# Decay exponents of the bidirectional SSD made by matmuls of 16 split rows, one exponential for both directions, and chunk rows loaded one chunk ahead

## The chip, the cores and the metric

The kernel runs on one core of one Trainium2 chip. The metric is the device time of one execution in microseconds, taken as the median over runs. The engines are PE (TensorE; PEld is its weight load), DVE (VectorE), ACT (ScalarE), POOL (GpSimd) and SP, which issues most DMAs.

## The reference

One encoder layer over 1280 tokens of width 1024 (a prompt of 256 and a sample of 1024, handled as one array of 10 chunks of 128 tokens). After a norm and an input projection, an S5 branch and a bidirectional Mamba-2 SSD branch run beside each other; gates merge them, and an MLP and a last norm follow. What the change touches is the SSD scan, run once forward and once backward over flipped inputs:

```python
da_cs = jnp.cumsum(dt * a.reshape(M2_GROUPS, k), axis=2)      # within a chunk of 128
xdt = x * dt[..., None]
lower = jnp.tril(jnp.ones((M2_CHUNK, M2_CHUNK), dtype=bool))[:, :, None, None]
seg = da_cs[:, :, :, None] - da_cs[:, :, None, :]
decay = jnp.exp(jnp.where(lower, seg, -jnp.inf))              # 128 x 128 for every head
cb = jnp.einsum('bclgn,bcsgn->bclsg', cm, bm)
y_diag = jnp.einsum('bclsg,bclsgk,bcsgkp->bclgkp', cb, decay, xdt)
...
y_off = jnp.einsum('bclgn,bcgkpn,bclgk->bclgkp', cm, prev, jnp.exp(da_cs))
```

There are 4 groups of 6 heads of 64 channels, and a state of 128.

## The kernel before, in words

Instructions are written in program order with priorities, and the framework's scheduler fixes at build time in which order each engine takes them. An engine runs its own list in order; a wait of one instruction holds up all that stand behind it. The same goes for the queue of DMAs on SP and that on ACT.

In order of time: the input projection for the S5 inputs, the S5 branch between further projection tiles (to about 560 us in the profiled execution), dt_proc (lines 344 to 421, near 540 to 605 us), the SSD stage, the two halves of the GLU (lines 624 to 657), merge and residual (to 1705 us), then the MLP.

**The SSD stage** runs over 4 groups j and 10 chunks k, 40 chunks in all. chunk_in (line 471) loads four 128x128 blocks of a chunk, transposes them on PE (line 477) and builds the backward state; chunk and chunk_out (lines 487 and 515) compute a chunk's output. The projection tiles for later groups and for gates (lists LATE, X, Z and TAIL) are emitted between the groups, and the scheduler lays their matmuls (mm3, line 129, tile mm) between those of the chunks on PE. The text calls these matmuls filler. The GLU's tiles lie in the memory of the projection's operands hh and hl, so the GLU starts when the last projection is done.

**One chunk before.** Line 523 makes the 128x128 product of B and C in bank ba; DVE multiplies it with both triangular masks into cb (line 525). ec holds the exponents for the carried states, broadcast over 64 partitions each from DRAM (line 531) and turned into exponentials (line 540). Then, for each half of three heads: cr, the sums of dt*a of both directions, is broadcast to 128 partitions by a DMA of 384 KB (line 550); ACT subtracts the per-partition sums, head by head (line 553); DVE does the other direction and takes the smaller of the two (line 556); ACT takes the exponential (line 558); ACT and DVE build the weights w, mask times dt for each direction, head by head (lines 561 and 562); DVE multiplies (line 563). Six matmuls give y (line 568). The per-partition sums and dt come from tiles ncs and dtt, transposed on PE in dt_proc (line 419).

PSUM banks in this stage: ps 2, ba 2, bk 1, y 1, and 2 for mm.

Of the kernel before, what the change touches and what calls it, by code (L numbers as in the profile page):

```python
# [8 lines left out]
F32 = mybir.dt.float32  # L9
# [9 lines left out]
P = 128  # L19
# [12 lines left out]
PB = (2, 2, 1, 1)  # L32
# [22 lines left out]
def tile_encoder(ctx: ExitStack, tc: tile.TileContext, a: dict, dbg=None):  # L55
# [44 lines left out]
    cs_d = dr.tile([10, 4, 2, 6, P], F32, name="cs_d")  # L100
# [56 lines left out]
    with ExitStack() as pctx:  # L157
# [184 lines left out]
        ncs, dtt, dst, dec = (kp.tile([P, 10, 48], F32, name=n) for n in ("ncs", "dtt", "dst", "dec"))  # L342

        def dt_proc():

            with tc.tile_pool(name="dtp", bufs=1) as dp:
# [68 lines left out]
                for src, dst_, sg in ((e, ncs, -1.0), (v, dtt, 1.0), (f, dst, 1.0)):  # L415
# [99 lines left out]
        def chunk_out(j, k, xt, sf, sb, ssum):  # L515
            bc = sp.tile([P, 2, P], F32, name="bc")
            nc.sync.dma_start(bc, xbc_d[5 * j + 3:5 * j + 5, :, cols(k)].rearrange("m p l -> p m l"))
            xz = sp.tile([P, 6, P], F32, name="xz", bufs=2)
            nc.sync.dma_start(xz, xz_d[j, :, :, cols(k)].rearrange("m p l -> p m l"))
            sz, xd = xz[:, 0:3], xz[:, 3:6]  # L520
# [25 lines left out]
            for hh_ in range(2):  # L546
                e = sp.tile([P, 3, P], F32, name="e", bufs=4)
                w = sp.tile([P, 3, P], F32, name="w", bufs=2)
                cr = sp.tile([P, 2, 3, P], F32, name="cr", bufs=2)
# [732 lines left out]
```

## Time and profile before

| | |
|---|---|
| median of 3 runs | 2617.65 us (2610.93 to 2621.97) |
| the profiled execution | 2624.81 us, its span 2623.0 us |
| PE busy | 2461.0 us, 94% of the span |
| DVE, ACT, POOL busy | 60%, 40%, 39% |
| granted clock of PE, mean | 0.979 of full speed |

A share over the whole span mixes stages. The last 918 us are the MLP, where PE has work all the time; the SSD stage lies between 618 us (first chunk) and 1283 us, and shares PE with filler.

### The profile page before, as it was taken

Reading aid. Unit: us, or ns where it says so; the run is one execution under the profiler, and the core shown is the slowest. Engines: PE = TensorE matmul, PEld = TensorE weight load, DVE = VectorE, ACT = ScalarE, POOL = GpSimd, SP = SyncE. Lnnn points to the kernel's source line nnn. Section 1 sums busy time; section 2 is a strip of 40 time slices with the busy share of each in tenths; the row PEclk is TensorE's granted clock in tenths of the full one; section 3 lists DMA queues with packets and bytes.
Section 4 is the critical chain, followed back from the end, with each engine's and each line's share of the span. In section 5 each row is a group of like instructions: output and inputs, shape, how many; then the busy total and the mean of one; then the engine's idle time right before and its main releaser. Section 6 shows DMA issues by size and latency. Waiting matters only on the chain.

```text
span 2623.0 us, 37529 instructions
## 1 busy us (share of the span) xinstructions
PE 2461.0 (94%) x13809; PEld 2094.9 (80%) x13809; DVE 1578.7 (60%) x2641; ACT 1052.0 (40%) x2308; POOL 1011.3 (39%) x790
## 2 busy tenths in 40 slices
PE   8899998798988999898899899999999999999998
PEld 6688877686866777676799898988888888888887
DVE  7799999786488786769752645433333333333336
ACT  7455555326566674666442434411111111111114
POOL 2511111122364553557644667632222232222235
PEclk9999999899999999998999999999999999999999
DMA  4323223226466665766556666531111111111113
GB/s 146 97 84 98 90 89 96 79 74 180 158 193 199 196 215 156 215 211 203 175 180 195 209 199 205 168 124 41 37 37 41 37 37 41 37 37 41 36 42 116
DMA packets 273656, 315.73 MB, mean 120 GB/s; under 512 B 30520, under 2 KB 206400, under 8 KB 273472
## 3 DMA queue, kind: packets, MB, share of 16 engines
q1 hardware_dynamic: 217984, 262.20, 32.1%
q10 hardware_dynamic: 55488, 51.13, 6.7%
q8 instruction: 109, 1.79, 0.3%
q14 instruction: 75, 0.61, 0.1%
HBM read 240.73 MB, written 72.52 MB: 119 GB/s over the span
## 4 chain that ended last, share of the span: by engine, by line
PE 56%; DVE 20%; DMA 9%; ACT 5%; issue 5%; POOL 3%; ACTq 0%; SPq 0%; DVEq 0%; POOLq 0%
PE pa L138 24%; PE mm L129 12%; PE pa L129 9%; PE mm L138 8%; DMA ec<-cs_d 3%; DMA cr<-cs_d 2%; POOL wl L114 2%; DVE ac L307 2%; DVE z L1127 1%; DVE z L1126 1%; DVE w L562 1%; DMA raw<-w_m 1%; PE ps L449 1%; PE y L568 1%; DMA wt<-w_d 1%
## 5 line engine op out<-in xcount | busy, mean ns | idle before, releaser
L114 POOL TENSOR_TENSOR wl<-raw,wh 128x512 fp32r<-128x512 f32 (+1 forms) x422 | 597.7, 1421 | 1317.6 <-ACT wh L113 1299.8
L113 ACT ACTIVATE wh<-raw 128x512 fp32r<-128x512 f32 (+1 forms) x422 | 258.1, 614 | 938.5 <-PE pa L138 523.0
L129 PE MATMUL mm<-hh,wl 128*128 128x512 f32 (+1 forms) x1272 | 472.5, 371 | 42.3 <-POOL wl L114 9.8
L129 PE MATMUL mm<-hl,wh 128*128 128x512 f32 (+1 forms) x1272 | 467.6, 368 | 0.1
L129 PE MATMUL mm<-hh,wh 128*128 128x512 f32 (+1 forms) x1272 | 467.5, 368 | 0.0
L129 PEld LDWEIGHTS mm<-hh,wl 128*128 128x128 f32 x1272 | 245.8, 193 | 88.6 <-POOL wl L114 14.5
L129 PEld LDWEIGHTS mm<-hl,wh 128*128 128x128 f32 x1272 | 246.1, 194 | 40.6 <-issue 1.8
L129 PEld LDWEIGHTS mm<-hh,wh 128*128 128x128 f32 x1272 | 245.4, 193 | 40.8 <-issue 3.6
L138 PE MATMUL pa<-hid,wh 128*128 128x512 f32 (+1 forms) x1008 | 254.6, 357 | 0.0
L750 DVE TENSOR_TENSOR acc<-acc,pa 128x512 f32<-128x512 f32 (+1 forms) x252 | 138.2, 594 | 140.5 <-PE pa L138 140.5
L138 PEld LDWEIGHTS pa<-hid,wh 128*128 128x128 f32 x1008 | 170.3, 188 | 29.8
L734 DVE SCALAR_TENSOR_TENSOR r<-pa,rs 128x512 f32<-128x512 f32 (+1 forms) x72 | 39.6, 596 | 230.0 <-PE pa L138 230.0
L129 PE MATMUL pa<-gx,wh 128*128 128x432 f32 (+1 forms) x576 | 158.5, 356 | 0.0
L138 PE MATMUL pa<-xnh,wl 128*128 128x512 f32 (+1 forms) x576 | 155.8, 357 | 0.0
L138 PE MATMUL pa<-xnl,wh 128*128 128x512 f32 (+1 forms) x576 | 155.0, 357 | 0.0
L138 PE MATMUL pa<-xnh,wh 128*128 128x512 f32 (+1 forms) x576 | 154.0, 357 | 0.0
L138 PE MATMUL pa<-hid,wl 128*128 128x512 f32 (+1 forms) x504 | 143.4, 355 | 0.0
L556 DVE SCALAR_TENSOR_TENSOR e<-cr,ncs,e 128x128 f32<-128x128 f32 x240 | 123.9, 562 | 28.6 <-ACT e L553 26.6
L562 DVE SCALAR_TENSOR_TENSOR w<-cb,dtt,w 128x128 f32<-128x128 f32 x240 | 116.0, 529 | 7.4 <-ACT w L561 7.4
L307 DVE SCALAR_TENSOR_TENSOR ac<-xpad,hcw,ac 128x1282 f32<-128x1282 f32 x60 | 100.8, 1679 | 21.8 <-ACT ac L305 21.5
L129 PEld LDWEIGHTS pa<-gx,wh 128*128 128x128 f32 x576 | 108.3, 188 | 3.6
L138 PEld LDWEIGHTS pa<-xnh,wh 128*128 128x128 f32 x576 | 96.5, 188 | 17.8
(449 smaller groups left out, 5071.7 us busy)
## 6 DMA issues: line engine op xcount, KB each, us to landing
cr<-cs_d ACTq DMA_DIRECT2D x80, 384.0 KB
raw<-w_in SPq DMA_DIRECT2D x110, 256.0 KB
raw<-w_m SPq DMA_DIRECT2D x72, 256.0 KB
raw<-w_dn SPq DMA_DIRECT2D x72, 256.0 KB
raw<-w_up SPq DMA_DIRECT2D x64, 256.0 KB
ec<-cs_d ACTq DMA_DIRECT2D x80, 192.0 KB
xz<-xz_d SPq DMA_DIRECT2D x40, 384.0 KB
raw<-w_o SPq DMA_DIRECT2D x48, 256.0 KB
```

The costliest lines, as they stand in the source:

```text
L113: act.activation(wh[:, :n], raw[:, :n], AF.Copy)
L114: pool.tensor_tensor(wl[:, :n], raw[:, :n], wh[:, :n], SUB)
L129: pe.matmul(out, l, r[:, sl], start=(n == 0), stop=(n == last))
L138: pe.matmul(o, l, r[:, sl], start=(n == 0), stop=(n == last))
L307: dve.scalar_tensor_tensor(ac[:, :n], xp[:, k:k + n], w(k), ac[:, :n], MUL, ADD)
L449: pe.matmul(st[:, :384], xt[:, 384:512], xs, start=True, stop=True)
L556: dve.scalar_tensor_tensor(e[:, h], cr[:, 1, h], ncs[:, k, 24 + r + h:25 + r + h], e[:, h], ADD, MIN)
L562: dve.scalar_tensor_tensor(w[:, h], cbu, b, w[:, h], MUL, ADD)
L568: pe.matmul(y[e0 * 64:e0 * 64 + 64, q * P:(q + 1) * P], xt[:, h * 64:h * 64 + 64], G[h // 3][:, h % 3], start=True, stop=True)
L734: dve.scalar_tensor_tensor(r[:, s], pt, 0.0, rs2[:, s], MAX, MUL)
L750: dve.tensor_tensor(ac[:, m, s], ac[:, m, s], pt, ADD)
L1126: dve.tensor_tensor_scan(z[lo, 2:n + 2], flat(dk)[lo], flat(src)[lo], 0.0, MUL, ADD)
```

## The change

The exponent of a head's 128x128 decay matrix is now written to PSUM by two accumulating matmuls for each direction and half of a chunk. The first multiplies the identity (eye) with a matrix that is 0 where the mask holds and -1e30 elsewhere (out_of), broadcast over three heads. The second has 16 contraction rows: el (weights) and er (moving) hold the running sums e and the values ln(dt) - e, each split into a high and a low fp32r part, and rows of constants that pick head and direction. One ACT exponential then covers both directions and three heads (768 values per partition); DVE adds the two directions and multiplies with cb. dt is inside the exponent, so w, ncs, dtt and cr are gone. cb is a plain copy by ACT. dt_proc stores the split rows in DRAM (cs_d, ns_d, es_d). A chunk's loads (bc, ec, er, el, xz) stand in chunk_loads and are written one chunk ahead of their use; ec moves from ACT's queue to SP's. The PSUM banks become ps 2, ba 1, ex 2 (one tile of two banks), y 1; the second carried-state product takes the bank y instead of bk.

```diff
-PB = (2, 2, 1, 1)
+PB = (2, 1, 1, 1)
...
-                for h in range(2):
-                    for j in range(4):
-                        for d in range(2):
-                            r = 64 * h + 32 * d + 6 * j
-                            nc.sync.dma_start(cs_d[5 * h:5 * h + 5, j, d].rearrange("k r l -> r k l"),
-                                              by_chunk(e[r:r + 6]))
+                def parts(src, dst_):
+                    hl2 = [T(f"{src.name}p{i}", F32R) for i in range(2)]
+                    act.activation(hl2[0], src, AF.Copy)
+                    dve.tensor_tensor(hl2[1], src, hl2[0], SUB)
+                    for i in range(2):
+                        for h in range(2):
+                            for d in range(2):
+                                r = 64 * h + 32 * d
+                                nc.sync.dma_start(dst_(i, d)[:, :, h * HT:h * HT + HT], hl2[i][r:r + 24].bitcast(F32))
+                for h in range(2):
+                    for d in range(2):
+                        r = 64 * h + 32 * d
+                        nc.sync.dma_start(es_d[:, d, :, h * HT:h * HT + HT], e[r:r + 24])
+                parts(e, lambda i, d: cs_d[:, d, i])
+                dve.tensor_scalar(q, v, 1e-37, None, MAX)
+                act.activation(q, q, AF.Ln)
+                dve.tensor_tensor(q, q, e, SUB)
+                parts(q, lambda i, d: ns_d[:, d, :, i])
...
-                for src, dst_, sg in ((e, ncs, -1.0), (v, dtt, 1.0), (f, dst, 1.0)):
+                for src, dst_, sg in ((f, dst, 1.0),):
...
+        def chunk_loads(j, k):
+            i = nth[0] % NR
+            nth[0] += 1
+            er, el = ers[i], els[i]
             bc = sp.tile([P, 2, P], F32, name="bc")
             nc.sync.dma_start(bc, xbc_d[5 * j + 3:5 * j + 5, :, cols(k)].rearrange("m p l -> p m l"))
+            ec = sp.tile([P, 2, 3, P], F32, name="ec")
+            rows = es_d[j, :, :, cols(k)].rearrange("d (q e) l -> e d q l", e=2)
+            for e0 in range(2):
+                nc.sync.dma_start(ec[e0 * 64:e0 * 64 + 64], rows[e0:e0 + 1].to_broadcast([64, 2, 3, P]))
+            nc.sync.dma_start(er[0:4].bitcast(F32), cs_d[j].rearrange("d i r t -> (d i) r t")[:, :, cols(k)])
+            nc.sync.dma_start(el[4:16].bitcast(F32), ns_d[j, :, :, :, cols(k)].rearrange("d r i l -> (r i) d l"))
...
         def chunk_out(j, k, xt, sf, sb, ssum):
+            i = 10 * j + k
+            for z in order[i:i + 2]:
+                if z not in ahead:
+                    ahead[z] = chunk_loads(*z)
+            bc, xz, ec, er, el = ahead.pop((j, k))
...
-            cb = sp.tile([P, 2, P], F32, name="cb")
-            dve.tensor_tensor(cb, ba[:, 384:512].unsqueeze(1).to_broadcast([P, 2, P]),
-                              C("low", 0, 2 * P).rearrange("p (i l) -> p i l", i=2), MUL)
+            cb = sp.tile([P, 1, P], F32, name="cb")
+            act.activation(cb[:, 0], ba[:, 384:512], AF.Copy)
...
-                bk = ba if not offs else place("bk", PB[2])
+                bk = ba if not offs else place("y", PB[3])
...
-                nc.scalar.dma_start(cr, cs_d[k, j, :, 3 * hh_:3 * hh_ + 3].unsqueeze(0).to_broadcast([P, 2, 3, P]))
-                r = 6 * j + 3 * hh_
-                for h in range(3):
-                    act.activation(e[:, h], cr[:, 0, h], AF.Identity, bias=ncs[:, k, r + h:r + h + 1])
-
-                for h in range(3):
-                    dve.scalar_tensor_tensor(e[:, h], cr[:, 1, h], ncs[:, k, 24 + r + h:25 + r + h], e[:, h], ADD, MIN)
-                ef = e.rearrange("p h l -> p (h l)")
-                act.activation(ef, ef, AF.Exp)
-                for h in range(3):
-                    f, b = (dtt[:, k, 24 * d + r + h:24 * d + r + h + 1] for d in range(2))
-                    act.activation(w[:, h], cbl, AF.Copy, scale=f)
-                    dve.scalar_tensor_tensor(w[:, h], cbu, b, w[:, h], MUL, ADD)
-                dve.tensor_tensor(e, e, w, MUL)
+                ps = pq.tile([P, 2, 512], F32, name="ex", bufs=1)[:, :, :384]
+                for d in range(2):
+                    pe.matmul(ps[:, d].rearrange("p (h l) -> p h l", h=3), eye, out_of[:, d:d + 1].to_broadcast([P, 3, P]),
+                              start=True, stop=False)
+                    pe.matmul(ps[:, d], el[:, d], er[:, 3 * hh_:3 * hh_ + 3].rearrange("p h l -> p (h l)"),
+                              start=False, stop=True)
+                e = sp.tile([P, 2, 384], F32, name="e", bufs=3)
+                act.activation(e, ps, AF.Exp)
+                dve.tensor_tensor(e[:, 0], e[:, 0], e[:, 1], ADD)
+                ev = e[:, 0].rearrange("p (h l) -> p h l", h=3)
+                dve.tensor_tensor(ev, ev, cb.to_broadcast([P, 3, P]), MUL)
```

On PE, in the third group of chunks, a chunk before reads like this (mm are filler, ps the transposes of a later chunk, ba and bk the products with the carried states, y the six output matmuls):

```order
L477 MATMUL ps<-cst,xf 128x128 x4
L523 MATMUL ba<-bc 128x128
L568 MATMUL y<-e,xt_8898 64x128
L538 MATMUL ba<-bc,sf 128x128 x3
L568 MATMUL y<-e,xt_8898 64x128 x5
L538 MATMUL bk<-bc,sb_8694 128x128 x3
L129 MATMUL mm<-hh_99,wh 128x512
L129 MATMUL mm<-hh_100,wl 128x512
L129 MATMUL mm<-hl_108,wh 128x512
```

After the change the same place holds blocks of four matmuls of 384 columns into ex, two blocks a chunk, between the others (lines of the changed kernel: 598 and 600 are ex, 611 is y, 587 the carried states, 133 filler):

```order
L587 MATMUL ba<-bc,sf 128x128 x3
L133 MATMUL mm<-hh_100,wl 128x512
L133 MATMUL mm<-hl_108,wh 128x512
L133 MATMUL mm<-hh_100,wh 128x512
L598 MATMUL ex<-out_of,eye 128x384
L600 MATMUL ex<-er_6047,el_6049 128x384
L598 MATMUL ex<-out_of,eye 128x384
L600 MATMUL ex<-er_6047,el_6049 128x384
L133 MATMUL mm<-hh_101,wl 128x512
L133 MATMUL mm<-hl_109,wh 128x512
L133 MATMUL mm<-hh_101,wh 128x512
L611 MATMUL y<-e,xt_9670 64x128 x3
```

Eight matmuls a chunk have come in, and none of PE's other work of a chunk has gone.

On DVE, also in the third group, before (e, w and cb as above; x6 is six instructions of 128x128):

```order
L571 TENSOR_TENSOR yt<-y,xz 128x384
L556 SCALAR_TENSOR_TENSOR e<-cr,ncs,e 128x128 x6
L525 TENSOR_TENSOR cb<-ba,cst 128x256
L541 TENSOR_TENSOR ec<-ec,ba 128x384
L571 TENSOR_TENSOR yt<-y,xz 128x384
L562 SCALAR_TENSOR_TENSOR w<-cb,dtt,w 128x128 x3
L563 TENSOR_TENSOR e<-e,w 128x384
L562 SCALAR_TENSOR_TENSOR w<-cb,dtt,w 128x128 x3
L563 TENSOR_TENSOR e<-e,w 128x384
```

and after, where a half has two instructions (lines 604 and 606):

```order
L604 TENSOR_TENSOR e<-e 128x384
L606 TENSOR_TENSOR e<-e,cb 128x384
L614 TENSOR_TENSOR yt<-y,xz 128x384
L473 TENSOR_TENSOR sb_9599<-sb_9599,ps 128x384
L590 TENSOR_TENSOR ec<-ec,ba 128x384
L604 TENSOR_TENSOR e<-e 128x384
L606 TENSOR_TENSOR e<-e,cb 128x384
L604 TENSOR_TENSOR e<-e 128x384
L606 TENSOR_TENSOR e<-e,cb 128x384
L590 TENSOR_TENSOR ec<-ec,ba 128x384
```

Fifteen DVE instructions of a chunk (six of line 556, six of line 562, two of line 563, one of line 525) have become four.

## Rows read from the trace of the kernel before

**Rows 1.** The page of the profile: busy time of engines, clock in slices.
```profile
span 2623.0 us, 37529 instructions
...
PE 2461.0 (94%) x13809; PEld 2094.9 (80%) x13809; DVE 1578.7 (60%) x2641; ACT 1052.0 (40%) x2308; POOL 1011.3 (39%) x790
...
PEclk9999999899999999998999999999999999999999
```

**Rows 2.** Windows by stage: busy us (count), granted clock, DMA share, GB/s.
```profile
core 0: us, PE busy (x) PEld busy (x) DVE busy (x) ACT busy (x) POOL busy (x), PEclk, DMA share, GB/s
...
560.00:618.00 58.00, 51.82 (x257) 43.04 (x256) 45.46 (x49) 24.39 (x51) 11.18 (x6) 0.97 0.48 135
618.00:1190.00 572.00, 529.93 (x2956) 420.73 (x2954) 417.95 (x812) 369.09 (x978) 279.01 (x270) 0.98 0.63 189
1190.00:1283.00 93.00, 72.11 (x433) 59.95 (x432) 82.05 (x136) 56.53 (x139) 76.15 (x65) 0.89 0.68 199
1283.00:1400.00 117.00, 109.47 (x724) 107.07 (x724) 54.38 (x78) 37.76 (x72) 53.44 (x48) 0.99 0.61 190
1400.00:1705.00 305.00, 292.65 (x1484) 276.79 (x1483) 152.69 (x188) 122.81 (x216) 196.47 (x143) 0.99 0.62 195
1705.00:2623.00 918.00, 907.12 (x4682) 767.37 (x4680) 337.42 (x578) 148.10 (x212) 271.19 (x186) 0.99 0.16 50
```

**Rows 3.** The chain, from the page, that ended last, shares of the span.
```profile
PE 56%; DVE 20%; DMA 9%; ACT 5%; issue 5%; POOL 3%; ACTq 0%; SPq 0%; DVEq 0%; POOLq 0%
PE pa L138 24%; PE mm L129 12%; PE pa L129 9%; PE mm L138 8%; DMA ec<-cs_d 3%; DMA cr<-cs_d 2%; POOL wl L114 2%; DVE ac L307 2%; DVE z L1127 1%; DVE z L1126 1%; DVE w L562 1%; DMA raw<-w_m 1%; PE ps L449 1%; PE y L568 1%; DMA wt<-w_d 1%
```

**Rows 4.** Waits of PE from 618 to 1400: total us, times, longest us.
```profile
engine line waited for: us in total, times, longest us
PE y L568 <- DVE e L563: 10.0, 10, 2.7
PE ps L449 <- ACT xs L440: 9.5, 3, 5.7
PE mm L129 <- ACT xpad L301: 7.5, 3, 4.3
PE ba L523 <- DMA bc<-xbc_d: 6.1, 4, 2.0
...
PE y L568 <- DVE yt L571: 3.7, 1, 3.7
```

**Rows 5.** Timeline of PE: start us, length us, like instructions in a row.
```profile
1039.72 0.39 PE L129 MATMUL mm<-hl,wh 128*128 128x512 f32 x1
...
1045.32 0.81 PE L449 MATMUL ps<-xs,xt 128*128 128x384 f32 x2
1045.96 0.60 PE L477 MATMUL ps<-cst,xf 128*128 128x128 f32 x4
1046.32 0.48 PE L129 MATMUL mm<-hl,wh 128*128 128x512 f32 x1
1046.64 0.40 PE L129 MATMUL mm<-hh,wh 128*128 128x512 f32 x1
...
1055.50 0.28 PE L129 MATMUL mm<-hh,wl 128*128 128x256 f32 x1
...
1056.82 0.38 PE L523 MATMUL ba<-bc 128*128 128x128 f32 x2
```

**Rows 6.** Groups of DVE, 618 to 1283: busy us, mean ns, idle before, releaser.
```profile
L556 DVE SCALAR_TENSOR_TENSOR e<-cr,ncs,e 128x128 f32<-128x128 f32 x234 | 122.0, 567 | 25.8 <-ACT e L553 25.4
L562 DVE SCALAR_TENSOR_TENSOR w<-cb,dtt,w 128x128 f32<-128x128 f32 x240 | 116.0, 529 | 7.4 <-ACT w L561 7.4
...
L563 DVE TENSOR_TENSOR e<-e,w 128x384 f32<-128x384 f32 x80 | 50.6, 637 | 0.7
L571 DVE TENSOR_TENSOR yt<-y,xz 128x384 f32<-128x384 f32 x40 | 21.9, 547 | 12.3 <-PE y L568 11.1 <-issue 0.9 <-DMA bc<-xbc_d 0.3
L541 DVE TENSOR_TENSOR ec<-ec,ba 128x384 f32<-128x384 f32 x40 | 21.7, 543 | 7.5 <-PE ba L538 7.3
...
L525 DVE TENSOR_TENSOR cb<-ba,cst 128x256 f32<-128x256 f32 x40 | 16.5, 413 | 5.5 <-PE ba L523 5.4
```

**Rows 7.** Groups of ACT, 618 to 1283, same columns.
```profile
L553 ACT ACTIVATE e<-cr,ncs 128x128 f32<-128x128 f32 x234 | 75.8, 391 | 24.3 <-DMA cr<-cs_d 16.5 <-PE y L568 3.2 <-PE mm L129 3.1
L561 ACT ACTIVATE w<-cb,dtt 128x128 f32<-128x128 f32 x240 | 75.6, 389 | 12.7 <-DVE e L563 10.3 <-DVE cb L525 1.9
...
L558 ACT ACTIVATE e<-e 128x384 f32<-128x384 f32 x79 | 40.2, 515 | 26.1 <-DVE e L556 25.9
...
L480 ACT ACTIVATE xt<-ps 128x512 f32<-128x512 f32 x40 | 23.3, 583 | 6.7 <-PE ps L477 6.7
...
L308 ACT ACTIVATE xpad<-ac 128x1282 f32<-128x1282 f32 x12 | 15.2, 1267 | 17.8 <-DVE ac L307 14.2 <-POOL yt L573 3.6
```

**Rows 8.** Waits of the queue on SP from 618 to 1283; then DMA issues.
```profile
SPq L575 <- POOL yt L574: 162.7, 36, 13.5
SPq L112 <- POOL wl L114: 100.5, 45, 10.9
...
SPq L517 <- PE ba L538: 38.1, 17, 8.9
...
q1 hardware_dynamic: 93555, 76.80, 38.0%
q10 hardware_dynamic: 53176, 49.31, 25.3%
...
cr<-cs_d ACTq DMA_DIRECT2D x76, 384.0 KB
ec<-cs_d ACTq DMA_DIRECT2D x76, 192.0 KB
```

More of the change, by code (lines that the diff above doesn't have):

```diff
@@ L31 @@
 NMM, NPA = 2, 6
-PB = (2, 2, 1, 1)
+PB = (2, 1, 1, 1)
+BIG = 1.0e30
 PI = math.pi
@@ L99, in tile_encoder @@
     xz_d = dr.tile([4, 6, P, NT], F32, name="xz_d")
-    cs_d = dr.tile([10, 4, 2, 6, P], F32, name="cs_d")
+    cs_d = dr.tile([4, 2, 2, 6, NT], F32, name="cs_d")
+    es_d = dr.tile([4, 2, 6, NT], F32, name="es_d")
+    ns_d = dr.tile([4, 2, 6, 2, NT], F32, name="ns_d")
     def urgent():
@@ L341, in tile_encoder @@
         kp = pctx.enter_context(tc.tile_pool(name="ssdk", bufs=1))
-        ncs, dtt, dst, dec = (kp.tile([P, 10, 48], F32, name=n) for n in ("ncs", "dtt", "dst", "dec"))
+        dst, dec = (kp.tile([P, 10, 48], F32, name=n) for n in ("dst", "dec"))
         def dt_proc():
@@ L513, in norm_factors @@
             nc.sync.dma_start(rs_d[j, k0:k0 + n], r)
-        def chunk_out(j, k, xt, sf, sb, ssum):
+        NR = 2
+        ers = [sp.tile([16, 6, P], F32R, name=f"er{i}", bufs=1) for i in range(NR)]
+        els = [sp.tile([16, 2, P], F32R, name=f"el{i}", bufs=1) for i in range(NR)]
+        for i in range(NR):
+            B6 = [16, 6, P]
+            pick = lambda o: ident[0:16, 4 + o:16 + o:2].unsqueeze(2).to_broadcast(B6)
+            dve.tensor_tensor(ers[i], pick(0), pick(1), ADD)
+            for d in range(2):
+                dve.tensor_tensor(els[i][:, d], *(ident[0:16, c:c + 1].to_broadcast([16, P]) for c in (2 * d, 2 * d + 1)), ADD)
@@ L516, in chunk_out @@
+        eye = sp.tile([P, P], F32R, name="eye", bufs=1)
+        dve.tensor_copy(eye, ident)
+        out_of = sp.tile([P, 2, P], F32R, name="out_of", bufs=1)
+        dve.tensor_scalar(out_of.rearrange("p i l -> p (i l)"), C("low", 0, 2 * P), BIG, BIG, MUL, SUB)
+        nth = [0]
+        def chunk_loads(j, k):
+            i = nth[0] % NR
+            nth[0] += 1
+            er, el = ers[i], els[i]
             bc = sp.tile([P, 2, P], F32, name="bc")
             nc.sync.dma_start(bc, xbc_d[5 * j + 3:5 * j + 5, :, cols(k)].rearrange("m p l -> p m l"))
-            xz = sp.tile([P, 6, P], F32, name="xz", bufs=2)
@@ new lines, in chunk_loads, with chunk_out @@
+            xz = sp.tile([P, 6, P], F32, name="xz")
+            nc.sync.dma_start(xz, xz_d[j, :, :, cols(k)].rearrange("m p l -> p m l"))
+            return bc, xz, ec, er, el
+        order = [(j, k) for j in range(4) for k in range(10)]
+        ahead = {}
+        def chunk_out(j, k, xt, sf, sb, ssum):
+            i = 10 * j + k
[3 more added lines that the diff above has]
+            bc, xz, ec, er, el = ahead.pop((j, k))
@@ L546, in chunk_out @@
             for hh_ in range(2):
-                e = sp.tile([P, 3, P], F32, name="e", bufs=4)
-                w = sp.tile([P, 3, P], F32, name="w", bufs=2)
-                cr = sp.tile([P, 2, 3, P], F32, name="cr", bufs=2)
-                nc.scalar.dma_start(cr, cs_d[k, j, :, 3 * hh_:3 * hh_ + 3].unsqueeze(0).to_broadcast([P, 2, 3, P]))
-                r = 6 * j + 3 * hh_
-                for h in range(3):
-                    act.activation(e[:, h], cr[:, 0, h], AF.Identity, bias=ncs[:, k, r + h:r + h + 1])
-                for h in range(3):
-                    dve.scalar_tensor_tensor(e[:, h], cr[:, 1, h], ncs[:, k, 24 + r + h:25 + r + h], e[:, h], ADD, MIN)
-                ef = e.rearrange("p h l -> p (h l)")
-                act.activation(ef, ef, AF.Exp)
-                for h in range(3):
-                    f, b = (dtt[:, k, 24 * d + r + h:24 * d + r + h + 1] for d in range(2))
-                    act.activation(w[:, h], cbl, AF.Copy, scale=f)
-                    dve.scalar_tensor_tensor(w[:, h], cbu, b, w[:, h], MUL, ADD)
-                dve.tensor_tensor(e, e, w, MUL)
-                G.append(e)
+                ps = pq.tile([P, 2, 512], F32, name="ex", bufs=1)[:, :, :384]
+                for d in range(2):
+                    pe.matmul(ps[:, d].rearrange("p (h l) -> p h l", h=3), eye, out_of[:, d:d + 1].to_broadcast([P, 3, P]),
[7 more added lines that the diff above has]
+                dve.tensor_tensor(ev, ev, cb.to_broadcast([P, 3, P]), MUL)
+                G.append(ev)
             y = place("y", PB[3])
```

5 lines of the change are left out of this document (removed).

## The prediction

> **What bounds the kernel now.** I read the page first: PE is busy 94% of the span and its weight load 80%, all other engines 60% or less [rows 1]. That is an average, so the second view is the windows by stage [rows 2]. From 1705 us on, the MLP, PE is busy 907 of 918 us; nothing of the change reaches it. The SSD stage, 618 to 1283 us, is the place to look. PE is busy 529.9 of 572.0 us until 1190 and 72.1 of 93.0 us after it; in the GLU that follows, 109.5 of 117.0 us. So PE idles 42.1, 20.9 and 7.5 us there, 70.5 us in all. DVE is nearly full too: 418 of 572 us, then 82 of 93 us. The chain gives PE 56% of the span and DVE 20%, with the loads ec and cr at 3% and 2% [rows 3]: in the SSD stage it changes hands often, and no single engine owns it. PE's own waits say the same [rows 4]: the longest total is 10.0 us for DVE's product e, then 9.5 us for ACT's weighted rows xs, 7.5 us for ACT emptying a filler bank, 6.1 us for the load bc. These are many short waits, not one long one.
>
> The reader is to see from this that PE's work is the budget. Filler (projection, then GLU) is the same in both kernels, it must be done before the merge, and PE does it whenever a chunk does not want it. The time of the stage is therefore PE's work plus PE's idle time plus what a low clock costs. A change that relieves DVE and ACT can take from idle time only; a change that adds matmuls adds to the work.
>
> The clock matters a little. The granted clock is 0.98, 0.89 and 0.99 of 2.4 GHz in the three windows [rows 2]. With two levels, 2.4 and 1.2 GHz, a share of 2 x (1 - 0.98) = 4% of 572 us, 22% of 93 us and 2% of 117 us was at the low one, some 45 us; if PE worked all through them it lost half, 22 us at most.
>
> **The change, part by part.** *Added on PE.* Two matmuls for each of 2 directions and 2 halves of 40 chunks: 320, of 384 columns each. The trace has no such matmul, but it has filler of the same type with 512 and 256 columns, back to back [rows 5]: between the starts at 1039.72 and 1045.32 stand 24 of 512, 233 ns each; between 1055.50 and 1056.82 stand 11 of 256, 120 ns each. Midway lies 177 ns, and 320 x 0.177 = 56.6 us. Half of them have only 16 contraction rows; no row shows whether that is cheaper. From below I take the four transposes of 128 columns in 0.36 us [rows 5], 90 ns each: 160 x 0.087 = 14 us less. From above, 233 ns for all: 18 us more. I take the middle, since it is the columns that set the two filler prices. The Trainium skill, TensorE: Matmul & The Clock Gate, section Back-to-back issue gap, states N/2.4 + 2.5 ns, which for 384 columns is 162.5 ns and for all of them 52 us (an estimate); for 512 columns it gives 216 ns where the row shows 233, so here the row decides. After a block of plain f32 matmuls the first filler matmul takes 0.32 us instead of 0.233 [rows 5]; the new blocks have the type of filler, so a block costs such a switch only where it splits f32 work. With half of 80 blocks doing so it is 40 x 0.09 = 4 us (0 to 7).
>
> *Removed on PE.* Ten transposes in dt_proc, about 0.09 us each: 1 us. Net PE work: 56.6 + 4 - 1 = 59.6 us.
>
> *DVE.* Lines 556, 562, 563 and 525 were 122.0 + 116.0 + 50.6 + 16.5 = 305 us [rows 6]. In their place come 160 instructions of 128x384, at the 547 ns of line 571 (PSUM source) to the 637 ns of line 563: 88 to 102 us. DVE loses some 205 us of its 500 us in the stage. *ACT.* Lines 553, 561 and 558 go, 75.8 + 75.6 + 40.2 = 192 us [rows 7]. The new exponential has 768 values: 515 ns for 384 and 1267 ns for 1282 give 0.84 us, times 80 is 67 us; with 40 copies of cb at 0.39 us, 16 us. ACT loses some 109 us. None of this counts by itself; it counts where PE waited for it.
>
> *Loads.* cr, 384 KB twice a chunk on ACT's queue, goes; two loads of 12 KB come, and ec moves to SP [rows 8]. The ACT queue held 25.3% of the DMA time of the stage. PE waited for a load only for bc, 6.1 us [rows 4], which now is asked for a chunk ahead. On SP's queue a store of yt waits for POOL 162.7 us in 36 waits, 4.5 us each, and the weights for POOL 100.5 us; the 160 issues that come in stand behind these waits. A chunk takes 665/40 = 16.6 us, so a load one chunk ahead bears such a wait: I take nothing, and price it as a rival.
>
> *dt_proc.* It gains two splits, a logarithm and more stores, some 7 instructions of about 0.8 us ahead of the first chunk. Filler lies there (PE is busy 51.8 of 58.0 us from 560 to 618 [rows 2]): nothing, and if that cover is gone, 5 us.
>
> *What comes back.* From 618 to 1190 PE idles 42.1 us. The wait for e (10.0) and bc (6.1) lose their cause, and ACT reaches filler banks earlier (7.5). Against that, ex is one tile: each of 80 blocks waits until the exponential of the block before has read it. ba has one bank instead of two, and the second carried-state product waits for the bank y. I take 15 us back, a third. From 1190 to 1283, where filler is thin and DVE is busy 88%, relief of DVE should show most: 15 of 20.9 us, and 6 us of clock. The GLU keeps its 7.5 us. Sum: 59.6 - 15 - 15 - 6 = +23.6 us.
>
> The profiled execution took 2624.8 us; with the change it would take 2648. It lies 7.2 us above the median of the runs, 2617.65, so the forecast on that basis is **2641 us**, slower by 0.9%. If nothing comes back it is 2677.
>
> **The rivals.** *It all fits (faster).* PE has room for 42.1 + 20.9 us of idle time between 618 and 1283 and up to 22 us of clock, 85 us. If the freed DVE and ACT let PE take all of it, the kernel ends 85 - 60 = 25 us earlier, 2593 us. For it: DVE is 88% busy in the worst window, and each of the largest waits has an engine at its end that loses work. It decides from 60 us given back on. A second reading puts the room no smaller: weight load is busy 420.7 of 572 us and 60.0 of 93 us, but 767.4 of 918 us in the MLP; 0.736 and 0.645 against 0.836 leave 12% of 572 and 23% of 93, 69 + 21 = 90 us. The Trainium skill, Perfetto Trace Analysis, section Identifying the Most-Contended Engine, says to judge PE's headroom by the busy share of its weight loads rather than of its matmuls; by that rule the added work fits and the time would be this rival's. Against it: the waits are short and spread over PE's list, and the new list has more places to wait.
>
> *The one ex bank stalls PE (slower still).* Place: the first matmul of each ex block. If it waits half an exponential, 0.42 us, in each of 80 blocks, 33 us come on top: 2674 us. It decides if ACT's list puts an exponential behind other work of that length. Against it: between the two blocks of a chunk stand several filler matmuls.
>
> *Chunk rows come late on SP's queue (slower still).* If one chunk in four waits 4.5 us for er or el, 45 us come on top: 2686 us. Against it: the 16.6 us of lead.
>
> *No difference.* The 16-row matmuls cost 90 ns and a little more idle time comes back: 59.6 - 14 - 40 = +6 us, 2624 us.
>
> **How the numbers follow.** 13 us, 0.5%, is about what a measurement can tell from no change here (the three runs span 11 us). Chances: the forecast with its own range of 2631 to 2660, 0.40; the ex bank 0.11; late rows 0.06; no difference 0.25; all fits 0.18. Faster than 2604.6 is the last, 0.18; same 0.25; slower 0.57. For 8 in 10 the range must reach into both sides: low 2602, from the faster rival with a fifth of its gain short, high 2686.
>
> **What the changed profile would show.** Lines 598 and 600 at 177 ns from start to start within a block, and PE's busy time in the stage up by about 60 us less the clock's part. PE's idle time until the merge near 40 us; waits of line 598 for ACT total a few us (the ex bank: over 30), of line 600 for a load near nothing (late rows: over 30). DVE near 300 us in the stage. The clock near 0.97 or above around the last chunks. The MLP's 918 us as before. The forecast is wrong if PE's idle time falls below 15 us, if the 384-column matmuls cost far from 177 ns, or if filler lands elsewhere, so that the GLU starts late with PE empty.

## The result

The changed kernel takes 2660.19 us (median of 4 runs, 2655.09 to 2665.59) against 2616.35 us for the kernel before in the same comparison: a ratio of 1.0158, with a 95% interval of 1.0139 to 1.0177. It is slower by 1.6%, where the forecast was 0.9%. The profiled execution of the changed kernel took 2656.96 us, 32 us more than that of the kernel before.

The page of the changed kernel, with the lines that answer to [rows 1] and [rows 3]:

```profile
PE 2549.2 (96%) x14119; PEld 2137.9 (81%) x14119; DVE 1425.0 (54%) x2213; ACT 950.5 (36%) x1864; POOL 998.8 (38%) x790
...
PEclk9999999999999999999999999999999999999999
...
PE 71%; DVE 17%; DMA 5%; ACT 3%; issue 3%; POOL 1%; SPq 0%; DVEq 0%; ACTq 0%; POOLq 0%
PE pa L142 24%; PE mm L133 20%; PE pa L133 8%; PE mm L142 8%; PE ex L600 2%; PE ps L466 2%; PE ex L598 2%; DVE ac L311 1%; PE y L611 1%; DVE z L1170 1%; DVE z L1169 1%; DMA raw<-w_m 1%; DMA wt<-w_d 1%; POOL wl L118 1%; PE ba L587 1%
```

PE is busy 96% of the span instead of 94%, the clock has no slice under nine tenths left, and the chain, which changed hands often before, is PE for 71% of the span instead of 56%. The new matmuls, lines 598 and 600, are in it with 2% each; the loads ec and cr are gone from it.

The windows by stage of the changed kernel, cut where its stages end (the columns are those of [rows 2]):

```profile
613.00:1190.00 577.00, 576.12 (x3050) 433.89 (x3047) 276.12 (x424) 270.59 (x584) 264.51 (x257) 1.00 0.45 138
1190.00:1283.00 93.00, 89.68 (x508) 65.54 (x508) 56.91 (x80) 39.43 (x74) 63.66 (x64) 0.98 0.51 154
1283.00:1436.00 153.00, 138.85 (x903) 135.53 (x902) 67.22 (x89) 51.62 (x98) 74.58 (x62) 0.96 0.55 172
...
1740.00:2655.00 915.00, 904.00 (x4665) 764.84 (x4663) 335.95 (x577) 146.54 (x209) 269.07 (x184) 0.99 0.15 50
```

From 613 to 1190 us PE now idles 0.9 of 577 us, and from 1190 to 1283 us 3.3 of 93 us, where [rows 2] had 42.1 and 20.9 us. Weight load, though, is busy 434 of 577 us, 0.75 of the time where it was 0.74 [rows 2]. The GLU is over, and the first matmul of the merge starts, at 1437 us instead of 1405 us; the MLP at the end is as long as before. So the time did not come from waits: PE had more to do and did it without a pause.

PE's waits in the changed kernel, from the first chunk to the end of the GLU, to be set beside [rows 4]:

```profile
PE mm L133 <- DVE t L699: 9.0, 5, 4.4
PE mm L133 <- ACT sx5h L154: 5.0, 1, 5.0
PE ba L578 <- DVE ec L590: 1.4, 1, 1.4
PE ba L578 <- DMA bc<-xbc_d: 1.0, 1, 1.0
...
PE y L587 <- DVE yt L614: 0.5, 1, 0.5
```

The two longest belong to the GLU. Of the SSD's own waits 1.4, 1.0 and 0.5 us are left. No wait of the ex blocks is in the list.

A budget of the stage settles where the time went. For every matmul on PE's timeline, from the first product of B and C to the first matmul of the merge, I took the time to the next start, without the idle time that the timeline shows before that start, and added it up by kind (us):

| kernel | stage | filler | SSD's f32 matmuls | ex matmuls | PE idle |
|---|---|---|---|---|---|
| before | 786.8 | 541.8 | 174.7 | 0 | 70.3 |
| changed | 823.9 | 539.1 | 154.7 | 111.8 | 18.3 |

The stage grew by 37 us: 111.8 us of new matmuls, less 52.0 us of idle time, less 20.0 us on the f32 matmuls of the chunks, less 2.7 us of filler. The new matmuls are twice as dear as the 56.6 us of the forecast. The timeline of PE shows one ex block between filler and the product for the next state (start, length):

```profile
1100.62 0.28 PE L133 MATMUL mm<-hh,wh 128*128 128x256 f32 x1
1100.74 0.34 PE L598 MATMUL ex<-out_of,eye 128*128 128x384 f32 x1
1101.01 0.44 PE L600 MATMUL ex<-er,el 16*128 16x384 f32 x1
1101.38 0.44 PE L598 MATMUL ex<-out_of,eye 128*128 128x384 f32 x1
1101.74 0.44 PE L600 MATMUL ex<-er,el 16*128 16x384 f32 x1
1102.12 0.91 PE L466 MATMUL ps<-xs,xt 128*128 128x384 f32 x2
```

Inside the block the starts are 270, 370, 360 and 380 ns apart, not 177. The weight loads of the same block:

```profile
1100.62 0.19 PEld L598 LDWEIGHTS ex<-out_of,eye 128*128 128x128 f32 x1
1101.00 0.18 PEld L600 LDWEIGHTS ex<-er,el 16*128 16x128 f32 x1 [0.19 <-issue]
1101.37 0.19 PEld L598 LDWEIGHTS ex<-out_of,eye 128*128 128x128 f32 x1 [0.19 <-issue]
...
1102.11 0.30 PEld L466 LDWEIGHTS ps<-xs,xt 128*128 128x128 f32 x2 [0.19 <-issue]
```

The load for the first identity matmul starts at 1100.62, with the matmul ahead of it, and is hidden. The load of the 16 rows starts at 1101.00, when the matmul before it has run through, and PE's weight load has idled 0.19 us before it; so it goes at the next steps too. A step is then the 177 ns of the columns plus some 190 ns, in which PE waits first for the matmul before to run through and then for the load, which nothing hides. The record of a matmul begins with its own load where that is not hidden; the first identity matmul, whose load was hidden, has only the first part, and its step is 270 ns. This reading was put to the test.

### The profile page after: what moved, and what is told of

It is laid out like the page before. It is cut to its first block, busy times and chain, and to the rows that moved or that the text cites. A ratio compares the mean times of both kernels' runs of the same rounds, so it can differ in the third digit from the quotient of the medians.

```text
span 2655.1 us, 37240 instructions
## 1 busy us (share of the span) xinstructions
PE 2549.2 (96%) x14119; PEld 2137.9 (81%) x14119; DVE 1425.0 (54%) x2213; ACT 950.5 (36%) x1864; POOL 998.8 (38%) x790
## 3 DMA queue, kind: packets, MB, share of 16 engines
q1 hardware_dynamic: 252528, 279.90, 33.6%
## 4 chain that ended last, share of the span: by engine, by line
PE 71%; DVE 17%; DMA 5%; ACT 3%; issue 3%; POOL 1%; SPq 0%; DVEq 0%; ACTq 0%; POOLq 0%
PE pa L142 24%; PE mm L133 20%; PE pa L133 8%; PE mm L142 8%; PE ex L600 2%; PE ps L466 2%; PE ex L598 2%; DVE ac L311 1%; PE y L611 1%; DVE z L1170 1%; DVE z L1169 1%; DMA raw<-w_m 1%; DMA wt<-w_d 1%; POOL wl L118 1%; PE ba L587 1%
## 5 line engine op out<-in xcount | busy, mean ns | idle before, releaser
L118 POOL TENSOR_TENSOR wl<-raw,wh 128x512 fp32r<-128x512 f32 (+1 forms) x422 | 584.1, 1388 | 1364.2 <-ACT wh L117 1311.7
L133 PEld LDWEIGHTS mm<-hh,wh 128*128 128x128 f32 x1272 | 243.7, 192 | 42.1 <-issue 6.3
L604 DVE TENSOR_TENSOR e<-e 128x384 f32<-128x384 f32 x80 | 59.5, 743 | 113.2 <-ACT e L603 113.0
L142 PEld LDWEIGHTS pa<-xnh,wl 128*128 128x128 f32 x576 | 96.6, 188 | 17.8
```

The costliest lines, as they stand in the source:

```text
L118: pool.tensor_tensor(wl[:, :n], raw[:, :n], wh[:, :n], SUB)
L133: pe.matmul(out, l, r[:, sl], start=(n == 0), stop=(n == last))
L142: pe.matmul(o, l, r[:, sl], start=(n == 0), stop=(n == last))
L604: dve.tensor_tensor(e[:, 0], e[:, 0], e[:, 1], ADD)
```

## The experiments

**Theory A**: a change between weights of 128 rows and weights of 16 rows keeps PE from loading ahead, some 190 ns each way. **Theory B**: the row count has nothing to do with it; the second matmul of a pair waits for the first, since both add into the same PSUM columns, or the broadcast operand out_of reads slowly.

### 128 rows

```diff
-        ers = [sp.tile([16, 6, P], F32R, name=f"er{i}", bufs=1) for i in range(NR)]
-        els = [sp.tile([16, 2, P], F32R, name=f"el{i}", bufs=1) for i in range(NR)]
+        KR = 128
+        ers = [sp.tile([KR, 6, P], F32R, name=f"er{i}", bufs=1) for i in range(NR)]
+        els = [sp.tile([KR, 2, P], F32R, name=f"el{i}", bufs=1) for i in range(NR)]
...
+            for z, n in ((ers[i], 6 * P), (els[i], 2 * P)):
+                dve.tensor_scalar(z.rearrange("p h l -> p (h l)"), cst[0:KR, 0:n], 0.0, None, MUL)
```

> el and er are padded with zero rows to 128 contraction rows; nothing else changes. In the changed kernel a matmul of an ex block follows the one before it by about 370 ns, not by the 177 ns of the prediction. Theory A (the change between weights of 128 rows and weights of 16 rows costs PE about 190 ns each way): all matmuls of a block fall to about 177 ns, the 320 of them from 112 us to about 57 us, and the kernel ends about 50 us earlier, near 2610 us, no slower than the kernel before. Theory B (the second matmul of a pair waits for the first because both add into the same PSUM columns, or the broadcast moving operand reads slowly): nothing changes, 2660 us.

Measured: 2619.75 us, ratio to the kernel before 0.9991 (0.9976 to 1.0006). The same 320 matmuls, with zeros in 112 rows, take 40 us off the changed kernel (44 us by the two ratios to the kernel before). PE's timeline of one block:

```profile
1098.37 0.34 PE L601 MATMUL ex<-out_of,eye 128*128 128x384 f32 x1
1098.54 0.34 PE L603 MATMUL ex<-er,el 128*128 128x384 f32 x1
1098.72 0.35 PE L601 MATMUL ex<-out_of,eye 128*128 128x384 f32 x1
1098.91 0.34 PE L603 MATMUL ex<-er,el 128*128 128x384 f32 x1
1099.08 0.39 PE L133 MATMUL mm<-hl,wh 128*128 128x512 f32 x1
```

and its weight loads:

```profile
1098.37 0.19 PEld L603 LDWEIGHTS ex<-er,el 128*128 128x128 f32 x1
1098.55 0.19 PEld L601 LDWEIGHTS ex<-out_of,eye 128*128 128x128 f32 x1
```

The steps are 170 to 190 ns, and each load starts together with the matmul before its own. Over the stage the ex matmuls take 64.3 us instead of 111.8. Theory B falls: the pairs still add into the same columns, and out_of is still broadcast. Not all of the 47.5 us reaches the end: PE's idle time goes from 18.3 to 30.3 us.

### 64 rows

The edit is that of the run before with KR = 64.

> As the run with 128 rows, but padded to 64 rows. Theory A (any change of the row count between weights): as the changed kernel, 370 ns a matmul and 2660 us. Theory A2 (only weights of few rows, 16 or 32, are slow to come in): 177 ns and 2610 us. Theory B: 2660 us.

Measured: 2659.98 us, ratio 1.0138 (1.011 to 1.0165), the time of the changed kernel. A block on PE's timeline:

```profile
1102.75 0.44 PE L603 MATMUL ex<-er,el 64*128 64x384 f32 x1
1103.12 0.44 PE L601 MATMUL ex<-out_of,eye 128*128 128x384 f32 x1
1103.49 0.44 PE L603 MATMUL ex<-er,el 64*128 64x384 f32 x1
```

The steps of 370 ns are back, and the ex matmuls take 111.7 us. So it is not that few rows are slow to load: 64 rows between weights of 128 cost what 16 do.

### Identity first

```diff
                 for d in range(2):
                     pe.matmul(ps[:, d].rearrange("p (h l) -> p h l", h=3), eye, out_of[:, d:d + 1].to_broadcast([P, 3, P]),
                               start=True, stop=False)
+                for d in range(2):
                     pe.matmul(ps[:, d], el[:, d], er[:, 3 * hh_:3 * hh_ + 3].rearrange("p h l -> p (h l)"),
```

> Within a block the two identity matmuls come first and then the two of 16 rows, so a block changes weights' row count twice instead of four times; the same work in all. Theory A: 80 x 2 x 0.19 = 30 us less, 2630 us, with two of the four steps in a block at 177 ns. Theory B (adding into the same columns right behind the first matmul): the pairs are now apart, all steps fall to 177 ns and the kernel to about 2610 us; if the broadcast operand is what is slow, no change, 2660 us.

Measured: 2637.37 us, ratio 1.0057 (1.0039 to 1.0076): 23 us off the changed kernel (26 by the ratios) with the same matmuls in another order. The ex matmuls take 82.7 us, 29 us less, as theory A asks (30 us); idle time gave 5 us of it back. Two of one kind now show as one row:

```profile
1100.55 0.51 PE L598 MATMUL ex<-out_of,eye 128*128 128x384 f32 x2
1100.89 0.60 PE L494 MATMUL ps<-cst,xf 128*128 128x128 f32 x4
...
1102.09 0.62 PE L601 MATMUL ex<-er,el 16*128 16x384 f32 x2
1102.64 0.50 PE L133 MATMUL mm<-hl,wh 128*128 128x512 f32 x1
```

Two identity matmuls, with f32 work behind them, take 0.34 us, two 16-row matmuls 0.55 us. Record by record these are 284 and 262 ns, and over the stage the medians are 280 and 263 ns: the first of a pair pays for its own load, which was not hidden, and the second waits to run through before weights of 128 rows are loaded.

### The 16-row matmuls alone

This kernel leaves out the mask (the identity matmuls), and its exponential has a scale of 0, so that every decay is 1.

```diff
-                    pe.matmul(ps[:, d].rearrange("p (h l) -> p h l", h=3), eye, out_of[:, d:d + 1].to_broadcast([P, 3, P]),
-                              start=True, stop=False)
                     pe.matmul(ps[:, d], el[:, d], er[:, 3 * hh_:3 * hh_ + 3].rearrange("p h l -> p (h l)"),
-                              start=False, stop=True)
+                              start=True, stop=True)
...
-                act.activation(e, ps, AF.Exp)
+                act.activation(e, ps, AF.Exp, scale=0.0)
```

> The identity matmuls that add the mask are left out (and the exponential gets a scale of 0, so that values stay finite); the two 16-row matmuls of a block stand alone behind each other. Theory A: the second follows the first by 177 ns, and each change to and from the 128-row work around costs about 0.19 us. If a 16-row matmul is slow by itself, they stand 370 ns apart. The span falls by 160 matmuls: about 2600 us by theory A.

Measured: 2599.79 us in its one run. On PE's timeline a pair of 16-row matmuls is one row:

```profile
1105.24 0.39 PE L578 MATMUL ba<-bc 128*128 128x128 f32 x2
1105.56 0.61 PE L598 MATMUL ex<-er,el 16*128 16x384 f32 x2
1106.10 0.50 PE L133 MATMUL mm<-hh,wh 128*128 128x512 f32 x1
1106.43 0.39 PE L133 MATMUL mm<-hh,wl 128*128 128x512 f32 x1
```

and the weight loads:

```profile
1105.56 0.29 PEld L598 LDWEIGHTS ex<-er,el 16*128 16x128 f32 x2
1106.10 0.19 PEld L133 LDWEIGHTS mm<-hh,wh 128*128 128x128 f32 x1 [0.25 <-issue]
```

From the start of the pair to the next filler it is 0.54 us, 278 and 263 ns (medians of all pairs 280 and 263): neither the 177 ns nor the 370 ns that were expected. The two loads together take 0.29 us, so the second runs while the first matmul does, and a 16-row matmul behind another does not wait. What is above 177 ns belongs to the two changes, and each falls on two matmuls. On the way in, 17 filler matmuls of 512 columns ahead of a pair had a median of 326 ns to the next start where 232 ns is usual, and the first of the pair takes some 100 ns more than 177. On the way out, the second of the pair takes 86 ns more, and the filler behind it 339 ns (median of 39; 0.33 us in the rows above) instead of 232. Either way it is some 190 ns, as theory A has it.

### Where did PE's waits go

In the version with 128 rows the work that was added is near the size of the forecast, so it was taken as the base. **Theory C**: PE's waits went because DVE and ACT lost work. **Theory D**: they went because the rows of a chunk are asked for one chunk ahead.

**Nothing asked for ahead** (on the version with 128 rows):

```diff
-            for z in order[i:i + 2]:
+            for z in order[i:i + 1]:
```

> The version with 128 rows, with each chunk's loads written at the chunk itself and no longer one chunk ahead. In that version PE idles about 30 us between 613 and 1390 us, where the kernel before idled 70. Theory C (PE's waits went because DVE and ACT lost work): the loads cost little, idle time stays within 10 us of 30 and the time near 2620 us. Theory D (they went because rows are asked for a chunk ahead): idle time goes back up by 20 us or more, 2640 us or above.

Measured: 2619.34 us, ratio 0.9996 (0.9979 to 1.0014), the same as with loads ahead; PE's idle time in the stage is 32.4 us against 30.3. Here theory C holds and theory D does not.

**The kernel before, with loads asked for ahead**:

```diff
+        def chunk_loads(j, k):
+            bc = sp.tile([P, 2, P], F32, name="bc")
...
+                nc.sync.dma_start(ec[e0 * 64:e0 * 64 + 64], rows[e0:e0 + 1].to_broadcast([64, 2, 3, P]))
...
+            return bc, xz, ec
...
+            for z in order[i:i + 2]:
+                if z not in ahead:
+                    ahead[z] = chunk_loads(*z)
+            bc, xz, ec = ahead.pop((j, k))
...
-                nc.scalar.dma_start(ec[e0 * 64:e0 * 64 + 64], rows[e0:e0 + 1].to_broadcast([64, 2, 3, P]))
```

> The kernel before, with bc, xz and ec asked for one chunk ahead on SP's queue, and nothing else of the change. Theory C: only the wait for bc (6.1 us) can go, 2610 to 2620 us. Theory D: 20 to 40 us less idle time, 2580 to 2600 us.

Measured: 2621.16 us, ratio 1.0011 (0.9999 to 1.0023). Loads ahead alone bring nothing; theory C allowed a small gain and theory D asked for 20 us or more, and there was none. PE's longest wait of this kernel from 613 to 1390 us, and its wait for bc:

```profile
PE y L579 <- DVE e L574: 22.5, 15, 3.9
...
PE ba L538 <- DMA bc<-xbc_d: 4.1, 3, 2.7
```

The wait for DVE's product e, 10.0 us in [rows 4], is 22.5 us here; that for bc falls only from 6.1 to 4.1 us. PE's idle time in the stage is 73.1 us, none less than before.

**DVE's load put back** (on the version with 128 rows; the result of the eight additions is not used):

```diff
+                for _ in range(4):
+                    dve.tensor_tensor(load[0], load[0], load[0], ADD)
                 dve.tensor_tensor(e[:, 0], e[:, 0], e[:, 1], ADD)
```

> The version with 128 rows, with 8 more additions of 128x384 in each chunk on DVE, in front of its own two steps; their result is not used. They put back about 180 to 205 us of DVE time, what the change took off. Theory C: PE's idle time between 613 and 1390 us goes from 30 us back to 50 us or more, and the kernel to 2640 us or above. Theory D: no change, 2620 us.

Measured: 2670.61 us, ratio 1.0188 (1.0173 to 1.0204), 51 us above its base. The additions took 744 ns each, some 230 us instead of the 180 to 205 us that were meant. Nor did they stay with their chunks: no instruction needs their result, and the scheduler laid all 320 of them between 597 and 1032 us. The windows from 613 to 1390 us of the version with 128 rows, and then of this one:

```profile
613.00:1390.00 777.00, 746.62 (x4393) 630.99 (x4392) 406.07 (x588) 358.16 (x754) 399.76 (x378) 0.98 0.50 152
```

```profile
613.00:1390.00 777.00, 702.27 (x4043) 579.22 (x4042) 594.60 (x879) 338.24 (x721) 412.50 (x358) 0.97 0.47 143
```

DVE goes from 406 to 595 us, which is also 40 us more than the 555 us of the kernel before in this window, and PE falls from 746.6 to 702.3 us busy, 74.7 us idle. Cut where the additions end, this kernel has:

```profile
613.00:1032.00 419.00, 367.16 (x2037) 292.81 (x2036) 411.01 (x599) 188.74 (x406) 222.76 (x172) 0.99 0.43 132
1032.00:1200.00 168.00, 168.00 (x973) 136.79 (x973) 71.77 (x126) 74.91 (x174) 76.43 (x83) 1.00 0.47 141
```

While DVE is busy 411 of 419 us, PE idles 52 us, where the version with 128 rows idles 9; once the additions are over, PE idles not at all for 168 us. PE's longest waits of this kernel:

```profile
PE ps L494 <- DVE sb L473: 7.2, 5, 3.0
PE ba L584 <- DVE ec L596: 6.1, 7, 1.9
PE y L619 <- DVE ec L596: 5.6, 5, 1.8
```

They are for DVE, 18.9 us together; the version with 128 rows has 2.6 us at these places. Theory D has fallen with the two runs before. Of theory C this run shows that a full DVE makes PE idle. It does not show that the load which the change took off did so: in the kernel before, DVE was busy 307 of the same 419 us, not 411, and PE idled 33 us there. That part is argued, and what ACT's relief or the shorter chain of a chunk did was not tried alone.

### The mask on DVE

The last kernel keeps the padding to 128 rows and takes the identity matmuls off PE: DVE adds the mask while it moves the exponents from PSUM to SBUF.

```diff
                 for d in range(2):
-                    pe.matmul(ps[:, d].rearrange("p (h l) -> p h l", h=3), eye, out_of[:, d:d + 1].to_broadcast([P, 3, P]),
-                              start=True, stop=False)
                     pe.matmul(ps[:, d], el[:, d], er[:, 3 * hh_:3 * hh_ + 3].rearrange("p h l -> p (h l)"),
-                              start=False, stop=True)
+                              start=True, stop=True)
                 e = sp.tile([P, 2, 384], F32, name="e", bufs=3)
-                act.activation(e, ps, AF.Exp)
+                h3 = lambda z: z.rearrange("p d (h l) -> p d h l", h=3)
+                dve.tensor_tensor(h3(e), h3(ps), out_of.unsqueeze(2).to_broadcast([P, 2, 3, P]), ADD)
+                act.activation(e, e, AF.Exp)
```

> The version with 128 rows, with the mask added by DVE (one addition of 768 values, PSUM to SBUF, before the exponential) and no identity matmuls. PE loses 160 matmuls, about 33 us; DVE gains 80 x about 0.95 = 76 us. Theory C with PE as the budget: if DVE, then near 440 of 670 us in the stage, stays clear of the level at which PE waits for it, the kernel ends 25 to 33 us earlier, about 2590 us, faster than the kernel before by 1%. If the added DVE step makes PE wait again, it gives back half or more: 2605 us or above.

Measured: 2595.46 us (2591.18 to 2595.92), ratio 0.9900 (0.9885 to 0.9914): 1.0% faster than the kernel before, and the fastest of this study that computes all of it. Its window, PE's longest wait and its wait for the new DVE step, 613 to 1390 us:

```profile
613.00:1390.00 777.00, 741.87 (x4384) 622.91 (x4382) 473.32 (x677) 364.09 (x763) 415.23 (x387) 0.98 0.52 160
```

```profile
PE mm L133 <- DVE t L700: 7.4, 6, 3.5
...
PE ex L599 <- DVE e L603: 3.2, 4, 1.2
```

DVE is at 473 of 777 us, between the 406 us of the version with 128 rows, where PE idled 30.3 us in the stage, and the 595 us with the added load, where it idled 74.5 us; the kernel before had 555 us and 70.3. Here PE idles 33.6 us. The ex matmuls fall by 27.5 us (64.3 to 36.8), not by 33, and DVE gains 67 us, not 76.

The budget of the stage for all of them, worked out as above (us):

| kernel | stage | filler | SSD's f32 | ex | PE idle | median |
|---|---|---|---|---|---|---|
| before | 786.8 | 541.8 | 174.7 | 0 | 70.3 | 2616.35 |
| changed | 823.9 | 539.1 | 154.7 | 111.8 | 18.3 | 2660.19 |
| 128 rows | 785.5 | 536.5 | 154.5 | 64.3 | 30.3 | 2619.75 |
| 64 rows | 826.5 | 539.9 | 154.9 | 111.7 | 20.0 | 2659.98 |
| identity first | 800.6 | 539.3 | 155.4 | 82.7 | 23.3 | 2637.37 |
| 128 rows, none ahead | 784.4 | 535.0 | 153.1 | 63.9 | 32.4 | 2619.34 |
| before, loads ahead | 791.2 | 543.6 | 174.5 | 0 | 73.1 | 2621.16 |
| 128 rows, DVE load | 839.0 | 541.7 | 158.6 | 64.1 | 74.5 | 2670.61 |
| 16 rows alone | 770.4 | 541.2 | 160.9 | 44.7 | 23.6 | 2599.79 |
| mask on DVE | 760.4 | 538.0 | 152.0 | 36.8 | 33.6 | 2595.46 |

The median is of each kernel's own comparison (16 rows alone: one run), in which the kernel before had 2616.35, 2623.06 and 2620.96 us.

## Why the prediction was right, and where it was not

**The frame held.** The forecast was slower, because PE's work is the budget and the change adds to it what idle time can't give back. The range and the sign held. That the stage is PE's work plus its idle time lies in how the table is made; what the runs add is that filler hardly changes from kernel to kernel (535.0 to 543.6 us), so that what comes in on PE comes on top. That the time fell into the range is in part luck: 51 us too little for the new matmuls stand against 45 us too little taken off elsewhere. By a sign that the forecast named itself, 384-column matmuls far from 177 ns, its account of the added work was wrong.

**The price of the new matmuls was mis-sized.** The term 320 x 0.177 = 56.6 us measured 111.8 us (160 steps of some 330 ns behind the identity matmuls, 160 of 370 ns behind the others), far outside the bounds of 14 us less and 18 us more. The step that failed was to price a matmul by its columns alone, from filler whose weights all have 128 rows. The lower bound asked whether 16 rows might be cheaper; that the change of rows could cost was not asked. A page that speaks of it was passed over: the Trainium skill, TensorEngine Tiling (Array Packing), section Key Properties, says that a change of tiling mode drains TensorE, and gives no price. If fewer rows are another mode, which no row shows, the trace agrees: the load waits for the matmul before it to run through, some 190 ns at each change of rows. The runs with 128 and 64 rows, identity first and 16 rows alone show that it is this change. With it gone the term is 64.3 us. A further part stands in the table under filler and f32: a filler matmul of 512 columns right behind a 16-row one steps 338 ns in the changed kernel (median of 34) and 232 ns with 128 rows; 86 such ends of a block at some 0.1 us are about 9 us.

The price could have been read in the kernel before, where the weights of y have 64 columns and those of filler and of the products around it 128:

```profile
951.33 0.40 PE L129 MATMUL mm<-hh,wh 128*128 128x512 f32 x1
951.65 0.65 PE L568 MATMUL y<-e,xt 128*64 128x128 f32 x6
951.65 0.41 PEld L568 LDWEIGHTS y<-e,xt 128*64 128x64 f32 x6 [0.37 <-issue]
```

Filler of 512 columns steps 327 ns ahead of y (median of 20 places without a wait) and 235 ns ahead of f32 work with weights of 128x128; a 128x128 product steps 205 ns ahead of y and 111 ns ahead of its like. By these rows a change in the columns of the weights costs as a change in their rows does.

**The term for switching from f32 work (4 us) has no ground in the rows.** In the kernel before a filler matmul of 512 columns behind the products ba and bk takes 320 ns instead of 232, but the last product before it takes 31 instead of 112: together 350 ns against 344. With 128 rows the ex matmuls stand 7.7 us above 56.6 us, and that holds the low clock and what else there is; they were not taken apart.

**Idle time came back more than forecast.** The forecast took 30 of 70.5 us; 52 us came back: 41 of it ahead of 1190 us, where 15 were taken, and 17.6 between 1190 and 1283 us, where 15 were taken, while the GLU idles 6.6 us more (153.0 - 138.85 = 14.2 against 7.5). Part of this is that PE had more to do: a wait that filler or an ex block covers is no idle time. With 128 rows, where PE had 47.5 us less to do, 40.0 us came back. The waits did not go with the earlier loads. That they went with DVE's and ACT's work fits all rows of the table; the run with DVE's load shows only that a full DVE brings such waits, and relief of ACT was not tried alone.

**The clock** rose from 0.89 to 0.98 in the window before 1283 us. Its part was forecast at 6 us and is some 14 us over the stage: by the granted clock 51 us of the stage lay at the lower level of 1.2 GHz before and 20 us after, and the steps there, set against steps of the same kind at 2.4 GHz, were 21 us longer in all before and 7 us after.

**A term was missing.** The f32 matmuls of the chunks took 20.0 us less, 154.7 instead of 174.7 us. All versions with ex blocks keep most of it, the one with DVE's load and 74.5 us of idle time too (158.6 us), so idle time does not explain it. Some 9 us are the clock: in the kernel before 85 of the f32 matmuls ran at 1.2 GHz with a mean step of 229 ns, against 127 ns for the others, and in the changed kernel 10 did. The other 11 us are the same work in another order on PE. The blocks of y, with their changes of shape, are entered 62 times instead of 74, which is a few us of it; the rest stays open.

**The sum.** The stage grew by 37 us where 23.6 were forecast: 51 us too little was added for ex (111.8 against 56.6 + 4), 22 us too little of idle time, 20 of f32 work and 3 of filler taken off, 6 us taken off for the clock (its gain is in the f32 work and the filler here) and 1 for transposes that lie ahead of the stage. The stage begins 5.5 us earlier than before (613.2 against 618.6 us), where the forecast took nothing or 5 us more for dt_proc, so that the profiled execution is 9 us above the forecast for it, 2648; the other 10 of the 19 us to the median are the distance of profiled executions from medians (7 us above it was assumed, the changed kernel's lies 3 us below it).

**DVE and ACT.** DVE's steps took 743 and 777 ns instead of the 547 to 637 taken, ACT's exponential 804 ns (0.84 taken) and the copy of cb 272 ns (0.39 taken). The means of DVE hide two groups: 102 of the 160 steps took 0.56 us on average, the other 58 took 0.7 to 1.9 us, and each of the 58 ran while POOL worked (so did 46 of the 102; whether POOL is the cause was not tried). DVE lost 167 us in the stage (500 to 333 us), not 205. The two lines with the longest waits:

```profile
L604 DVE TENSOR_TENSOR e<-e 128x384 f32<-128x384 f32 x80 | 59.5, 743 | 113.2 <-ACT e L603 113.0
```

```profile
L603 ACT ACTIVATE e<-ex 128x768 f32<-128x768 f32 x80 | 64.3, 804 | 75.1 <-PE ex L600 61.9 <-issue 11.6 <-PE y L611 1.5
```

DVE waits 113 us for ACT's exponential and ACT 61.9 us for PE: the order of who waits is turned round, and PE is now waited for. One reading of the prediction does not hold, though nothing rests on it: the 25.3% of ACT's queue [rows 8] are a share of the 16 DMA engines' time, not of what they were busy.

**The rivals.** The ex bank did not stall PE: PE's list has no wait of line 598 for ACT. Chunk rows did not come late: line 600 waited for el 0.5 us in all, and the version with 128 rows does as well without loads ahead. The rival in which it all fits had the mechanism of the room right, 85 us: 59 us of idle time before 1283 us and some 14 us of clock came back; it fell on the price of what was to fit. The weight-load share, read as room, was 0.736 from 618 to 1190 us before and is 434/577 = 0.75 in the changed kernel, with PE busy 576 of 577 us. The Trainium skill, Perfetto Trace Analysis, section Identifying the Most-Contended Engine, would still read a quarter as headroom here; the trace does not agree, since PE had no room left; part of the missing share is the 0.19 us that PE's weight load idles before a load of an ex block.

## What to carry to other kernels

Before a small-contraction matmul is set between full ones, count the changes of the weights' shape, not only the columns: padding with zero rows cost nothing here and took 40 us off, and putting like next to like took 23 us off. Where PE's work plus its idle time makes a stage, relief of another engine is worth at most the idle time that it causes, so relief that is paid for on PE has to be cheaper than that; with the mask on DVE, which had room, the kernel was faster than the one before and than the version with 128 rows. Whether PE's idle time hangs on another engine can be tried by loading that engine, but look in the trace where the added work went: here it all ran in the first half of the stage.

## What the runs showed of the hardware that was not expected

Weights of 128 rows behind weights of 128 rows are loaded while the matmul before runs (steps of 170 to 190 ns with 384 columns, loads of 0.19 us hidden). Weights of 16 or 64 rows next to weights of 128 are not: their load starts when the matmul before has run through, and inside a block a step becomes 360 to 370 ns, in both directions. Such a change costs some 190 ns in two parts: the matmul before it steps some 90 ns longer (filler of 512 columns 326 instead of 232 ns), the first one behind it some 100 ns longer (filler 338 instead of 232 ns). The first part shows as well where the weights go from 128 to 64 columns (filler ahead of y 327 ns). Between two weights of 16 rows the load is hidden again, two loads in 0.29 us. The Trainium skill, TensorE: Matmul & The Clock Gate, section The mechanism, says in its list of what overlaps that a weight load overlaps with matmuls in flight only when it goes to other row groups; the trace differs here, hidden with the same 128 rows and not hidden where the row count changes. The text ahead of that list also lets a load go ahead into a background weight buffer; with that the hidden loads agree, though no row shows the buffer.
